# 128-row logit passes, side-by-side compressed blocks and forget gates beside the values in a two-layer hybrid trunk

## The chip, the cores and the metric

The kernel runs on one core of a Trainium2 chip. The metric is device time in microseconds of one execution; the median of three runs of the kernel before is 1275.02 us (1274.71 to 1275.39). Engines are named as in the profile: PE is TensorE's matmul, PEld its load of the stationary operand, DVE is VectorE, ACT ScalarE, POOL GpSimd and SP SyncE, which issues the transfers.

## The reference

A trunk of two layers over 512 positions of width 1024, float32 throughout.

```python
def reference(x, ...):
    h = x
    for layer in range(2):
        hn = rmsnorm(h, mix_norm[layer])
        if layer == 0: h = h + moba_nsa_mixer(hn, ...)
        else:          h = h + fox_mixer(hn, ...)
        h = h + sqrelu_mlp(rmsnorm(h, mlp_norm[layer]), mlp_w1[layer], mlp_w2[layer])
    return rmsnorm(h, final_norm)
```

Layer 0 projects the input once and splits the columns. Eight MoBA heads (width 64) attend causally to blocks of 256 keys, which at 512 positions is causal attention to all keys of the chosen blocks. Eight NSA heads in two key groups have three branches each, weighted by sigmoid gates: compressed keys (31 blocks of 32 positions, stride 16, each pressed through a small MLP `silu(blocks @ w1) @ w2` with hidden width 256), selected blocks and a sliding window. A relative-position bias is added to all these logits. Layer 1 has sixteen forgetting heads: `q k / 8 + cum[q] - cum[k]`, where `cum` is the running sum of `log_sigmoid(h @ w_f + b)` over positions, one column of `w_f` per head. Each mixer ends in an output projection, and an MLP of width 4096 with squared ReLU follows each.

## The kernel before, in words

**Numbers.** Every float32 matrix is split into a rounded part and a rest (`hi` and `lo`, type fp32r), and a product is three matmuls, hi x hi, lo x hi and hi x lo (`mm3`, L129 to L131). `split` (L91 on DVE or POOL, L88 on ACT) makes the two parts of a weight piece of at most 1024 columns per partition; the strings `MIX0_LOW` and `FOX_LOW` say, piece by piece, whether DVE (D) or POOL (P) computes the rest.

**Attention.** For each head, `softmax` (L261) makes the logits of four 128-query rows of 128, 256, 384 and 512 keys. In mixer 0 a row takes two passes over PE: q is stacked as hi in one half of the partitions and lo in the other (`QS`), k as hi in both halves (`KS`), so that one 128-row matmul gives hi x hi + lo x hi. The second pass, hi x lo, uses 64 rows: the hi half of `QS` and the matching half of `KL`, the rest of k. For NSA both halves of `KL` are filled already (`stack_k`, then a DVE subtraction and a POOL rounding), for MoBA one `KL` tile holds the two heads of a pair, one in each half. Then DVE adds the bias and takes the minimum (L265), ACT exponentiates (L266), DVE inverts the sum (L267), POOL normalizes (L268), PE transposes in pieces of 128 (L283), ACT and DVE split the result into `PTh` and `PTl` (L285, L286), and PE multiplies by the values (L295, L296). Probability tiles `P` come from a pool of three, transposed ones from pools of two, PSUM tiles `s`, `pt`, `o`, `acc` from two banks each.

**The compressed branch.** `compress_blocks` builds, for k and for v, the 31 blocks of both groups as 16 chunks of 62 columns, with a rounded tile `rh` and a rest `rl`. `compress_hidden` multiplies each chunk (a stationary tile of 128 columns, of which 62 count) by the weights of 256 columns in three passes. `compress_act` applies SiLU to the 62 x 256 result and transposes it; `compress_out` makes compressed keys `kcc` and values `vcs`, the values repeated in four strips of 32 partitions, one for each head of the group. `cmp_probs` computes the compressed softmax of four heads at once in a tile `cb` of its own. In `nsa_pair` each head multiplies its strip of 32 partitions by `vcs` (L510, L511, 32-row matmuls at a tile position).

**The forget gates.** `forget` in layer 1 loads the 16 gate columns (L951), pads them with zeros to 128 per chunk, splits them (L954, L955) and projects them like the queries, 24 matmuls of 512 columns with `fzh` and `fzl`. It then adds the bias, takes the logarithm and the running sum, and writes rows to memory (`fox_rows`) that the heads' `Q2` and `K2` tiles (68 rows) read. `values(0)`, which stands just before it in `FOX_ORDER`, projects the first 256 value columns for four position tiles.

**Order.** `MIX0_CMP`, `MIX0_ORDER` and `FOX_ORDER` give the order in which the parts are written. A scheduler of the framework then places the instructions on each engine by data, free buffers and priority; attention heads have a high one, so that projections and output projections fill in between. Each engine works its queue in that order.

Of the kernel before, what the change touches and what calls it, by code (L numbers as in the profile page):

```python
# [33 lines left out]
FOX_LOW = "DDPDDDPPPDPDPDDDDPPDPDDDPDPDPDPDD"  # L34
# [11 lines left out]
class Trunk:  # L46
# [278 lines left out]
    def band_setup(self, pool):  # L325

        nc, I = self.nc, self.I
        rb = self.sm.tile([32, 16], F32, tag="rb", name="rb")
        nc.sync.dma_start(rb, I["rel_bias"])
        tb = self.sm.tile([33, 16], F32, tag="tb", name="tb")  # L330
# [42 lines left out]

    def flat(self, v):
        return v.rearrange("p a b -> p (a b)")

    def mixer0(self):
# [5 lines left out]
        with ExitStack() as cx:  # L383
# [5 lines left out]
            self.pL = pool("l0L", 5)  # L389
# [49 lines left out]
            vcs = [a1.tile([P, 2, HD], FR, tag=f"vc{g}", name=f"vc{g}") for g in range(2)]  # L439
            nk = {}  # L440
            with tc.tile_pool(name="cmp", bufs=1) as cp:
# [17 lines left out]
                def nsa_k():  # L459
# [6 lines left out]
                    for g, r in enumerate((lo, hi)):  # L466
                        o_ = hi if g == 0 else lo
                        for bi in range(2):
                            ks = self.stack_k(pss[bi], r)
                            kl = self.pL.tile([P, S], FR, tag="KL", name=self.nm("KL"))  # L470
                            self.sub(kl[r], pss[bi][r], ks[r])
                            self.round(kl[o_], kl[r].bitcast(F32))
                            nk[bi, g] = (ks, kl)

                for s in MIX0_CMP.split():
# [9 lines left out]
                    else:  # L485
# [4 lines left out]
                        if part == 1:  # L490
                            hid[c] = self.compress_act(hid[c], cp)
                self.compress_out((hid[0], hid[1]), cp, kcc, vcs)
            vcf = [self.flat(v) for v in vcs]
# [6 lines left out]
            def nsa_pair(g, i, qs, ptc):  # L500
                o = o2.tile([P, S], F32, tag="o", name=self.nm("o"))
                for jj, r in enumerate((lo, hi)):
                    j = 2 * i + jj
                    head = 4 * g + j
                    with self.prio():
                        b = self.band(8 + head)
                        po = self.psum("o")
                        rr = slice(32 * j, 32 * j + 32)
                        tp = (32 * j, 0)
                        nc.tensor.matmul(po, vcf[g][rr], ptc[0][rr], start=True, stop=False, tile_position=tp)  # L510
                        nc.tensor.matmul(po, vcf[g][rr], ptc[1][rr], start=False, stop=False, tile_position=tp)  # L511
# [8 lines left out]
            def moba_qk(i):  # L520
# [8 lines left out]
                with self.tc.high_priority(offset=0):  # L529
                    ks = [self.stack_k(psk, r) for r in (lo, hi)]  # L530
                    kl = self.pL.tile([P, S], FR, tag="KL", name=self.nm("KL"))
# [4 lines left out]
            def moba_pair(i, qs, ks, kl):  # L536
# [45 lines left out]
    def compress_blocks(self, rg, c, cp):  # L582
# [12 lines left out]
        rh = self.pPT.tile([P, PTW], FR, tag="PTh", name=self.nm("rh"))  # L595
# [481 lines left out]
```

## Time and profile before

| | |
|---|---|
| median of three runs | 1275.02 us |
| the profiled execution | 1274.85 us, its span 1273.1 us |
| granted TensorE clock, mean | 0.997 |
| mixer 0 | 0 to about 332 us of the span |
| first MLP | to about 674 us |
| forgetting layer | to about 920 us |
| second MLP and final norm | to the end |
| busy in the span | PE 1244.3, DVE 957.4, ACT 656.5, POOL 457.9 us |

The profile is of one execution. A row of the timeline gives the start in us from the span's beginning, the duration, the engine, the line, the operation, the written tile <- the read tiles, and for PE the rows * columns of the stationary tile and the moving operand's shape; in brackets stands the idle time before it and what ended it. Matmuls overlap, so their durations add up to more than the time that passes: what one costs is read from the next one's start. A row of the windows gives the stretch, its length, then for each engine the busy time and number of instructions, the granted clock, and the transfers' share and rate. A row of waits names who waited for whom, the total in us, how often, and the longest.

### The profile page before, as it was taken

The page shows a single profiled execution, that of the slowest core. Times are in us where ns is not written, and L with a number is a line of the kernel's source. Part 1 is how long each engine was busy: PE and PEld are TensorE (multiplying, and loading weights), DVE is VectorE, ACT ScalarE, POOL GpSimd, SP SyncE. Part 2 cuts the span into 40 slices and gives each one's busy share as a digit, 9 for nine tenths or more (in the row PEclk, how much of TensorE's full clock was granted, in tenths as well). Part 3 has the DMA queues.
Part 4 walks back from the last instruction along what each step waited for, and adds up shares of the span by engine and source line. Part 5 has one row for each costly group of instructions (what it writes and reads, how often), then busy time and mean ns, then how long its engine had stood idle before and what let it go on. Part 6 is the DMA issues. An engine that isn't in the chain of part 4 may idle for free.

```text
span 1273.1 us, 17191 instructions
## 1 busy us (share of the span) xinstructions
PE 1244.3 (98%) x6254; PEld 1033.7 (81%) x6254; DVE 957.4 (75%) x1626; ACT 656.5 (52%) x1168; POOL 457.9 (36%) x462
## 2 busy tenths in 40 slices
PE   6999999999999999999999999999999999999996
PEld 6787877677888888888888889898798888888885
DVE  6766567767887889888877576647897888889885
ACT  5435565666465544554524676545455445444543
POOL 1534535443253332333201554525326233332313
PEclk9999999999999999999999999999999999999999
DMA  9762132122243332343205212222344324332301
GB/s 264 248 201 70 50 103 72 51 61 90 72 128 115 100 113 87 98 118 113 68 3 136 75 52 68 70 83 67 116 119 130 100 83 133 99 96 88 99 1 66
DMA packets 142048, 124.30 MB, mean 98 GB/s; under 512 B 6363, under 2 KB 116987, under 8 KB 141964
## 3 DMA queue, kind: packets, MB, share of 16 engines
q1 hardware_dynamic: 141964, 123.21, 32.8%
q8 instruction: 49, 0.80, 0.3%
q14 instruction: 35, 0.29, 0.1%
HBM read 120.79 MB, written 7.64 MB: 101 GB/s over the span
## 4 chain that ended last, share of the span: by engine, by line
PE 95%; DVE 3%; ACT 1%; DMA 0%; issue 0%; SPq 0%; DVEq 0%; ACTq 0%
PE acc L129 18%; PE acc L131 18%; PE acc L130 18%; PE s L856 12%; PE o L856 6%; PE s L261 6%; PE pt L283 4%; PE pt L856 3%; PE o L295 2%; PE o L296 2%; PE pt L232 1%; DVE whl L91 1%; PE s L131 1%; PE s L129 1%; PE s L130 1%; PE o L130 1%
## 5 line engine op out<-in xcount | busy, mean ns | idle before, releaser
L131 PE MATMUL acc<-xhi,whl 128*128 128x512 f32 (+1 forms) x784 | 301.0, 384 | 0.0
L130 PE MATMUL acc<-xlo,whl 128*128 128x512 f32 (+1 forms) x784 | 300.2, 383 | 0.0
L129 PE MATMUL acc<-xhi,whl 128*128 128x512 f32 (+1 forms) x784 | 299.9, 383 | 0.0
L91 DVE TENSOR_TENSOR whl<-raw,whl 128x1024 fp32r<-128x1024 f32 (+1 forms) x112 | 156.7, 1402 | 77.1 <-ACT whl L88 72.7
L759 POOL TENSOR_TENSOR r<-r,yrow 128x512 f32<-128x512 f32 x64 | 93.9, 1467 | 321.5 <-ACT r L758 319.1
L129 PEld LDWEIGHTS acc<-xhi,whl 128*128 128x128 f32 x784 | 147.4, 188 | 28.8 <-issue 1.3
L131 PEld LDWEIGHTS acc<-xhi,whl 128*128 128x128 f32 x784 | 147.5, 188 | 28.3 <-issue 0.5
L130 PEld LDWEIGHTS acc<-xlo,whl 128*128 128x128 f32 x784 | 147.6, 188 | 28.0 <-issue 0.7
L856 PE MATMUL s<-whl,sp 128*128 128x512 f32 x672 | 168.0, 390 | 0.0
L88 ACT ACTIVATE whl<-raw 128x1024 fp32r<-128x1024 f32 (+1 forms) x143 | 149.3, 1048 | 31.4 <-PE acc L131 11.8
L856 PEld LDWEIGHTS s<-whl,sp 128*128 128x128 f32 x672 | 126.2, 188 | 26.3
L811 DVE TENSOR_TENSOR whl<-w,whl 128x1024 fp32r<-128x1024 f32 x98 | 136.0, 1400 | 8.5 <-ACT whl L810 8.4
L810 ACT ACTIVATE whl<-w 128x1024 fp32r<-128x1024 f32 x98 | 102.4, 1059 | 72.6 <-PE s L856 42.3
L266 ACT ACTIVATE P<-P,sst 128x128 f32<-128x128 f32 (+3 forms) x160 | 88.9, 557 | 49.0 <-DVE sst L265 48.5
L758 ACT ACTIVATE r<-acc 128x512 f32<-128x512 f32 x62 | 37.1, 598 | 120.9 <-PE acc L131 120.9
L816 DVE TENSOR_TENSOR w<-w,w 128x1024 f32<-128x1024 f32 x56 | 91.2, 1629 | 9.0 <-DMA w<-in_mlp_w 8.1
L91 POOL TENSOR_TENSOR whl<-raw,whl 128x1024 fp32r<-128x1024 f32 (+2 forms) x31 | 75.1, 2425 | 62.8 <-ACT whl L88 51.2
L285 ACT ACTIVATE PTh<-pt 128x512 fp32r<-128x512 f32 (+1 forms) x120 | 61.3, 524 | 60.2 <-PE pt L283 58.9
L286 DVE TENSOR_TENSOR PTl<-pt,PTh 128x512 fp32r<-128x512 f32 (+1 forms) x120 | 70.5, 597 | 25.6 <-ACT PTh L285 24.7
L856 PE MATMUL o<-whl,sp 128*128 128x512 f32 x336 | 88.8, 390 | 0.0
L864 DVE TENSOR_TENSOR x<-s,x 128x512 f32<-128x512 f32 x112 | 75.1, 681 | 3.0 <-PE s L856 3.0
L268 POOL TENSOR_SCALAR P<-P,sst 128x128 f32<-128x128 f32 (+1 forms) x96 | 51.9, 546 | 67.5 <-DVE sst L267 66.1
(226 smaller groups left out, 2417.5 us busy)
## 6 DMA issues: line engine op xcount, KB each, us to landing
raw<-in_mlp_w SPq DMA_DIRECT2D x72, 512.0 KB
w<-in_mlp_w SPq DMA_DIRECT2D x56, 512.0 KB
raw<-in_odd_w_in SPq DMA_DIRECT2D x24, 512.0 KB
raw<-in_even_w_in SPq DMA_DIRECT2D x20, 512.0 KB
band<-bias_dram SPq DMA_DIRECT2D x24, 256.0 KB
bias_dram<-bias_rows SPq DMA_DIRECT2D x16, 320.0 KB
raw<-in_even_w_out SPq DMA_DIRECT2D x8, 512.0 KB
raw<-in_odd_w_out SPq DMA_DIRECT2D x8, 512.0 KB
```

What stands on the lines that cost most here:

```text
L88: i0 = nc.scalar.activation(hl[:, 0, :n], raw[:, :n], AF.Copy)
L91: i1 = eng.tensor_tensor(hl[:, 1, :n], raw[:, :n], hl[:, 0, :n].bitcast(F32), op=ALU.subtract)
L129: mm(ps, ahl[0], bhl[0], start=first, stop=False)
L130: mm(ps, ahl[0], bhl[1], start=False, stop=False)
L131: mm(ps, ahl[1], bhl[0], start=False, stop=last)
L261: nc.tensor.matmul(ps[:, :w], q[:, qi * P:(qi + 1) * P], k[:, :w], start=i == 0, stop=i == len(passes) - 1)
L266: nc.scalar.activation(seg, seg, AF.Exp, bias=mn, scale=-1.0, accum_out=sm)
L759: nc.gpsimd.tensor_tensor(r, r, row, op=ALU.mult)
L810: nc.scalar.activation(t[:, 0], src, AF.Copy)
L811: nc.vector.tensor_tensor(t[:, 1], src, t[:, 0].bitcast(F32), op=ALU.subtract)
L816: nc.vector.tensor_tensor(out, a_, b_, op=op)
L856: mm = lambda l, r, first, last: nc.tensor.matmul(ps, l, r, start=first, stop=last, skip_group_check=True)
```

## The change

Four things change.

1. The second logit pass in mixer 0 uses all 128 rows: `QS` (hi and lo halves) against a `KL` tile that holds the rest of k in both halves, so that lo x lo is added too. A helper `stack_kl` makes such a tile for each head; MoBA pairs have two tiles instead of one, and their pool grows from five to six. To make room, `cb` comes from the pool of probability tiles, and small tiles move to other pools.
2. In the compressed branch the rounded part and the rest of a chunk stand side by side in one stationary tile (62 + 62 columns), so that two passes (weights hi, weights lo) make four products. The two halves of the result are added after the transposition, in `compress_act`, and SiLU follows there.
3. The compressed values are laid out per head as 128 rows, zero outside the head's strip, so that the 32-row matmuls become 128-row ones without a tile position.
4. The forget gates' 16 columns are loaded with the first 256 value columns (three weight pieces instead of two) and projected with them, 272 columns; the 16 gate columns are copied to `zt` and transposed (L966) for the rest of `forget`.

```diff
-FOX_LOW = "DDPDDDPPPDPDPDDDDPPDPDDDPDPDPDPDD"
+FOX_LOW = "DDDPDDDPPPDPDPDDDDPPDPDDDPDPDPDPDD"
...
+    def stack_kl(self, ps, r, ks):
+        o = slice(HD, P) if r.start == 0 else slice(0, HD)
+        kl = self.pL.tile([P, S], FR, tag="KL", name=self.nm("KL"))
+        self.sub(kl[r], ps[r], ks[r])
+        self.round(kl[o], kl[r].bitcast(F32))
+        return kl
...
-            self.pL = pool("l0L", 5)
+            self.pL = pool("l0L", 6)
...
-                        rr = slice(32 * j, 32 * j + 32)
-                        tp = (32 * j, 0)
-                        nc.tensor.matmul(po, vcf[g][rr], ptc[0][rr], start=True, stop=False, tile_position=tp)
-                        nc.tensor.matmul(po, vcf[g][rr], ptc[1][rr], start=False, stop=False, tile_position=tp)
+                        nc.tensor.matmul(po, vcf[g][j], ptc[0], start=True, stop=False)
+                        nc.tensor.matmul(po, vcf[g][j], ptc[1], start=False, stop=False)
...
-                            p = self.softmax([(qs[j], ks), (qs[j][r], kl[r])], b, gates[:, :, 3 * head + 1 + bi])
+                            p = self.softmax([(qs[j], ks), (qs[j], kl)], b, gates[:, :, 3 * head + 1 + bi])
...
-                    kl = self.pL.tile([P, S], FR, tag="KL", name=self.nm("KL"))
-                    for r, k in zip((lo, hi), ks):
-                        self.sub(kl[r], psk[r], k[r])
-                return qs, ks, kl
+                    kls = [self.stack_kl(psk, r, k) for r, k in zip((lo, hi), ks)]
+                return qs, ks, kls
...
-                        p = self.softmax([(qs[j], ks[j]), (qs[j][r], kl[r])], b, None)
+                        p = self.softmax([(qs[j], ks[j]), (qs[j], kls[j])], b, None)
...
-        self.round(rh[:, :W + 66], rf[:, :W + 66])
-        nc.vector.tensor_tensor(rl[:, :W + 66], rf[:, :W + 66], rh[:, :W + 66].bitcast(F32), op=ALU.subtract)
-        return rh, rl
+        for hh, t in enumerate(rhl):
+            nc.gpsimd.memset(t[:, V:V + 4].bitcast(F32), 0.0)
+            tv = t[:, :V].rearrange("p (c h n) -> p c h n", c=8, h=2)
+            src = rf[:, hh * V // 2:(hh + 1) * V // 2].rearrange("p (c n) -> p c n", c=8)
+            self.round(tv[:, :, 0], src)
+            nc.vector.tensor_tensor(tv[:, :, 1], src, tv[:, :, 0].bitcast(F32), op=ALU.subtract)
+        return rhl
...
-            self.mm3(ps[:, :256], (rh[:, a], rl[:, a]), wc[k], cc == 0, cc == 15)
+            a = blocks[part][:, k * 124:k * 124 + P]
+            mm(ps[:, :256], a, wc[k][0], start=cc == 0, stop=False)
+            mm(ps[:, :256], a, wc[k][1], start=False, stop=cc == 15)
...
+        sg = cp.tile([124, 256], F32, tag="sg", name=self.nm("sg"))
+        nc.scalar.activation(sg, ps[:124, :256], AF.Copy)
...
+        nc.scalar.activation(z, pv[:, :, 62:124], AF.Copy)
+        nc.vector.tensor_tensor(z, pv[:, :, :62], z, op=ALU.add)
+        nc.scalar.activation(e, z, AF.Exp, scale=-1.0)
...
+            nc.gpsimd.memset(vcs[g].bitcast(F32), 0.0)
+            for j in range(4):
+                r = slice(32 * j, 32 * j + 32)
+                nc.scalar.activation(vcs[g][r, j, 0], pvv[r, :HD], AF.Copy)
+                self.sub(vcs[g][r, j, 1], pvv[r, :HD], vcs[g][r, j, 0])
...
-        cb = b1.tile([P, 4, 4, 32], F32, tag="cb", name=self.nm("cb"))
+        cb = self.pP.tile([P, PTW], F32, tag="P", name=self.nm("cb"))[:, :S].rearrange("p (q h n) -> p q h n", q=4, h=4)
...
-            wv = self.cols(w, [(2048, 2304)])
+            wv = self.cols(w, [(2048, 2304), (3072, 3088)])
...
-                    self.proj_n(ps, wc, 256, x, t)
+                    self.proj_n(ps, wc, 272 if c == 0 else 256, x, t)
+                    if c == 0:
+                        nc.vector.tensor_copy(zt[:, t], ps[:, 256:272])
...
-                nc.vector.tensor_tensor(fl, fr, fh.bitcast(F32), op=ALU.subtract)
-                psz = self.psum("acc")
-                for k in range(KD):
-                    self.mm3(psz, (fh[:, k], fl[:, k]), (x[0][:, k], x[1][:, k]), k == 0, k == KD - 1)
+                psz = self.psum("pt")
+                for t in range(NT):
+                    nc.tensor.transpose(psz[:16, t * P:(t + 1) * P], zt[:, t], self.ident)
```

The change moves few instructions. On PE the order of the attention heads stays the same but for one place, the MoBA heads at the time of the second compressed softmax. These are PE's rows there before, from a head's first product with the values (`vm`) on; `s` are logits, `acc` a projection:

```order
L296 MATMUL o_1968<-PTl_1948,vm_249 128x512
L131 MATMUL acc_2249<-xhi_122,whl_2246 128x512
L129 MATMUL acc_2249<-xhi_122,whl_2246 128x512
L130 MATMUL acc_2249<-xlo_123,whl_2246 128x512
L261 MATMUL s_2117<-KS_1651,QS_1615 128x128
L261 MATMUL s_2117<-KL_1657,QS_1615 128x128
L261 MATMUL s_2124<-KS_1651,QS_1615 128x256
L261 MATMUL s_2124<-KL_1657,QS_1615 128x256
```

And now the rows that stand between the last of the 18 projection matmuls that follow the same product and the head's first logits:

```order
L130 MATMUL acc_2288<-xlo_123,whl_2285 128x512
L295 MATMUL o_1971<-PTh_1950,vm_250 128x384
L131 MATMUL acc_2288<-xhi_122,whl_2285 128x512
L129 MATMUL acc_2288<-xhi_122,whl_2285 128x512
L283 MATMUL pt_2016<-ident,P_1984 128x128 x4
L296 MATMUL o_1971<-PTl_1951,vm_250 128x384
L283 MATMUL pt_2023<-ident,P_1984 128x128 x4
L295 MATMUL o_1971<-PTh_1950,vm_252 128x128
L296 MATMUL o_1971<-PTl_1951,vm_252 128x128
L295 MATMUL o_1971<-PTh_1950,vm_251 128x256
L296 MATMUL o_1971<-PTl_1951,vm_251 128x256
L261 MATMUL s_2120<-KS_1651,QS_1615 128x128
```

The head's logits (`QS_1615`) stood three projection matmuls behind that product and now stand behind 20 of them and the rest of the previous head.

At the forgetting layer's start DVE has these rows before, between the last two additions of the MLP (L898) and the third normalized tile:

```order
L955 TENSOR_TENSOR fzl<-fzr,fzh 128x1024
L898 TENSOR_TENSOR x_120<-o_6060,x_120 128x512
L171 SCALAR_TENSOR_TENSOR nrm_6164<-nrm_6164 128x1
L91 TENSOR_TENSOR whl_6100<-raw_6095,whl_6100 128x1024
L237 TENSOR_TENSOR xlo_6106<-pt_6121,xhi_6105 128x4x128
L237 TENSOR_TENSOR xlo_6106<-pt_6128,xhi_6105 128x4x128
L204 SCALAR_TENSOR_TENSOR xn_6163<-x_118,nrm_6164,g_6103 128x512 x2
```

And now, from the last addition (L909) on:

```order
L909 TENSOR_TENSOR x_120<-o_6069,x_120 128x512
L91 TENSOR_TENSOR whl_6114<-raw_6105,whl_6114 128x816
L91 TENSOR_TENSOR whl_6117<-raw_6108,whl_6117 128x544
L237 TENSOR_TENSOR xlo_6123<-pt_6138,xhi_6122 128x4x128
L237 TENSOR_TENSOR xlo_6123<-pt_6145,xhi_6122 128x4x128
```

The split of the gate weights (`fzl`) is gone, and two of the three smaller value pieces stand ahead of the normalized input's rest (`xlo`) in place of one.

More of the change, by code (lines that the diff above doesn't have):

```diff
@@ L327, in band_setup @@
         nc, I = self.nc, self.I
[L328 removed]
+        rb = pool.tile([32, 16], F32, tag="rb", name="rb")
         nc.sync.dma_start(rb, I["rel_bias"])
[L330 removed]
+        tb = pool.tile([33, 16], F32, tag="tb", name="tb")
         nc.vector.memset(tb, -NEG)
@@ L438, in mixer0 @@
             kcc = a1.tile([P, 2, 2, 2, 32], FR, name="kcc")
-            vcs = [a1.tile([P, 2, HD], FR, tag=f"vc{g}", name=f"vc{g}") for g in range(2)]
+            vcs = [a1.tile([P, 4, 2, HD], FR, tag=f"vc{g}", name=f"vc{g}") for g in range(2)]
             nk = {}
@@ L490, in mixer0 @@
                         if part == 1:
-                            hid[c] = self.compress_act(hid[c], cp)
+                            hid[c] = self.compress_act(hid[c], c, cp)
                 self.compress_out((hid[0], hid[1]), cp, kcc, vcs)
-            vcf = [self.flat(v) for v in vcs]
+            vcf = [[self.flat(v[:, j]) for j in range(4)] for v in vcs]
             self.pB = pool("l0B", 2)
@@ L594, in compress_blocks @@
         rf = self.pP.tile([P, PTW], F32, tag="P", name=self.nm("rf"))
-        rh = self.pPT.tile([P, PTW], FR, tag="PTh", name=self.nm("rh"))
-        rl = self.pPT.tile([P, PTW], FR, tag="PTl", name=self.nm("rl"))
-        nc.gpsimd.memset(rf[:, W:W + 66], 0.0)
+        rhl = [self.pPT.tile([P, PTW], FR, tag=tg, name=self.nm("rhl")) for tg in ("PTh", "PTl")]
+        V = 8 * 4 * NB
         rv = rf[:, :W].rearrange("p (c g n) -> p c g n", c=16, g=2)
@@ L640, in compress_out @@
             w2.append(t)
-        hkt = cp.tile([P, 2, 62], F32, name="hkt")
-        for f in range(2):
-            nc.vector.tensor_copy(hkt[:, f], hk[:, f * P:f * P + 62])
         pk = self.psum("o")
         for f in range(2):
-            nc.tensor.matmul(pk[:, :62], w2[0][:, f], hkt[:, f], start=f == 0, stop=f == 1)
+            nc.tensor.matmul(pk[:, :62], w2[0][:, f], hk[:, f], start=f == 0, stop=f == 1)
         nc.vector.memset(kcc.bitcast(F32), 0.0)
@@ L689, in cmp_probs @@
                 nc.vector.tensor_tensor(cbh, src, cbh, op=ALU.add)
-        st = self.sm.tile([P, 2, 16], F32, tag="cst", name=self.nm("cst"))
+        st = b1.tile([P, 2, 16], F32, tag="cst", name=self.nm("cst"))
         cv = cb.rearrange("p q h n -> p (q h) n")
@@ L946, in forget @@
                 ft = lambda pool_, tag, name, dt: pool_.tile([P, PTW], dt, tag=tag, name=name)
-                kv = lambda t_: t_[:, :KD * P].rearrange("p (k c) -> p k c", k=KD)
-                fr, fh, fl = (kv(ft(p_, t_, n_, d_)) for p_, t_, n_, d_ in (
-                    (self.pP, "P", "fzr", F32), (self.pPT, "PTh", "fzh", FR), (self.pPT, "PTl", "fzl", FR)))
-                nc.gpsimd.memset(fr, 0.0)
-                nc.sync.dma_start(fr[:, :, :16], w.rearrange("(k p) c -> p k c", p=P)[:, :, 3072:3088])
                 bf = a1.tile([16, 1], F32, name="bforget")
                 nc.sync.dma_start(bf, I["odd_b_forget"][0].rearrange("(h o) -> h o", o=1))
-                nc.scalar.activation(fh, fr, AF.Copy)
-                nc.vector.tensor_tensor(fl, fr, fh.bitcast(F32), op=ALU.subtract)
-                psz = self.psum("acc")
-                for k in range(KD):
-                    self.mm3(psz, (fh[:, k], fl[:, k]), (x[0][:, k], x[1][:, k]), k == 0, k == KD - 1)
+                psz = self.psum("pt")
+                for t in range(NT):
+                    nc.tensor.transpose(psz[:16, t * P:(t + 1) * P], zt[:, t], self.ident)
                 ze = ft(self.pP, "P", "ze", F32)
```

33 lines of the change are left out of this document (14 added, 19 removed).

## The prediction

> **What bounds the kernel now.** First the page: busy time and the chain of waits.
>
> ```profile
> span 1273.1 us, 17191 instructions
> PE 1244.3 (98%) x6254; PEld 1033.7 (81%) x6254; DVE 957.4 (75%) x1626; ACT 656.5 (52%) x1168; POOL 457.9 (36%) x462
> PE 95%; DVE 3%; ACT 1%; DMA 0%; issue 0%; SPq 0%; DVEq 0%; ACTq 0%
> ```
>
> TensorE ends nearly every wait. Busy PE is not yet useful PE, though, because a matmul's row includes its pipeline's tail. So next comes the timeline, where what counts is the distance from one start to the next. Here is a stretch of mixer 0 that contains logit rows (KS,QS is the first pass, KL,QS the second, 64 rows), and then one of the forgetting layer.
>
> ```profile
> 201.79 0.36 PE L296 MATMUL o<-PTl,vm 128*128 128x256 f32 x1
> 202.08 0.44 PE L261 MATMUL s<-KL,QS 64*128 64x384 f32 x1
> 202.46 0.50 PE L261 MATMUL s<-KS,QS 128*128 128x512 f32 x1
> 202.89 0.50 PE L261 MATMUL s<-KL,QS 64*128 64x512 f32 x1
> 203.32 0.50 PE L130 MATMUL acc<-xlo,whl 128*128 128x512 f32 x1
> 203.65 0.40 PE L131 MATMUL acc<-xhi,whl 128*128 128x512 f32 x1
> ...
> 720.95 0.97 PE L261 MATMUL s<-K,Q 128*128 128x384 f32 x4
> 721.76 0.40 PE L131 MATMUL acc<-xhi,whl 128*128 128x512 f32 x1
> 721.99 0.39 PE L129 MATMUL acc<-xhi,whl 128*128 128x512 f32 x1
> ```
>
> A 512-column matmul between others of 128 rows takes 0.23 us (721.76 to 721.99). The four logit matmuls of the forgetting layer (two of 384 columns, two of 512) take 0.81 us, so 384 columns take (0.81 - 0.46)/2 = 0.175 us. In mixer 0 the matmuls that start at 202.08 should then end at 202.08 + 0.175 + 3 x 0.23 = 202.95; the next one starts at 203.65. So 0.70 us are lost around two 64-row passes: 0.35 us each, half of it before the next 128-row pass, half before the 64-row pass. Third, the chain of waits of the two attention stretches (95 to 330, then 690 to 920), the windows, and who waits in mixer 0.
>
> ```profile
> by line: PE s L261 21.7%; PE acc L129 15.8%; PE acc L130 15.2%; PE acc L131 15.1%; PE pt L283 12.7%; PE o L295 7.6%; PE o L296 7.3%; PE o L510 1.3%; DVE x L322 0.9%; PE o L511 0.8%; PE s L674 0.7%; PE pt L705 0.4%; DVE o L302 0.3%; ACT o L3
> by line: PE acc L129 24.4%; PE acc L131 24.2%; PE acc L130 24.2%; PE s L261 8.7%; PE pt L283 7.7%; PE o L296 4.4%; PE o L295 4.3%; DVE whl L91 1.2%; issue 0.6%; DVE x L322 0.3%; PE pt L232 0.1%; DVEq L91 0.0%; DVEq L223 0.0%
> 95.00:320.00 225.00, 225.00 (x1168) 172.12 (x1167) 150.96 (x449) 134.49 (x327) 99.66 (x145) 1.00 0.24 71
> DVE P L265 <- PE s L261: 32.7, 36, 4.3
> ACT PTh L285 <- PE pt L283: 38.9, 31, 4.0
> PEld s L261 <- issue: 15.5, 67, 0.4
> ```
>
> L261 is 21.7% of 235 us, 51.0 us for 96 pairs of passes, against 8.7% of 230 us, 20.0 us for 64 pairs: 0.53 us a pair against 0.31. From 95 to 320 PE never stops, and VectorE (150.96) and ScalarE (134.49 of 225) wait for it. That stretch is bound by PE, and part of its PE time is the passage between tile heights.
>
> **The 128-row logit passes.** 96 64-row matmuls become 96 of the same width with 128 rows. The forgetting layer's passes have 128 and 68 rows by turns and pay only for columns, so the added rows cost nothing and the gain is the lost time. From the chain it is 0.22 us a pair, 21.0 us; from starts 0.35, 33.6 us; with the wait ahead of the first of them (201.79 to 202.08 is 0.29 where 256 columns should take 0.12, rows below) it is 0.70 + 0.17 for two passes, 0.44, or 42 us. I take 33.6, because starts are measured and the chain's ends are modelled, and because neighbouring pairs share a passage. The whole will not come out: where softmaxes stand without projections between them, the vector engines come next.
>
> ```profile
> 230.00:240.00 10.00, 10.00 (x43) 6.08 (x42) 7.71 (x29) 6.84 (x20) 7.22 (x8) 1.00 0.43 134
> 280.00:300.00 20.00, 20.00 (x101) 13.80 (x101) 14.88 (x62) 15.83 (x46) 8.83 (x16) 1.00 0.24 64
> ...
> 230.00:240.00 10.00, 4.99 (x14) 2.66 (x14) 1.00 0.43 134
> 280.00:300.00 20.00, 10.63 (x33) 6.15 (x33) 1.00 0.24 64
> ...
> 674.00:690.00 16.00, 12.85 (x95) 12.21 (x93) 14.19 (x26) 7.48 (x13) 4.60 (x4) 0.89 0.56 149
> ```
>
> The second pair of rows counts L261 alone: 33 passes in 280 to 300, so 16.5 x 0.35 = 5.8 us to be had, leaving 14.2 us of PE against 15.83 of ScalarE. How full can an engine get? From 674 to 690, where VectorE holds up PE, it was busy for 14.19 of 16 us, 89%. By that, 280 to 300 shrinks to 15.83/0.89 = 17.8, 3.6 us less than hoped; 230 to 240 shrinks to 7.71/0.89 = 8.7 instead of 7.55, 1.1 us less. Over the whole stretch VectorE's 151 would be 79% of 225 - 34 us, below that. Another 2.3 us I take off as an estimate (half of 18 x 0.23 = 4.1 us) for the softmax that the order moves behind 18 projection matmuls: it comes out later, where there is less cover. What is left: 33.6 - 7.0 = **26.6 us**.
>
> This part adds eight rounds of KL on POOL and a KL tile per head. The nearest row:
>
> ```profile
> L250 POOL TENSOR_SCALAR KL<-KL 64x512 fp32r<-64x512 f32 x4 | 5.1, 1272 | 0.6 <-DVE KL L244 0.3
> ```
>
> 8 x 1.27 = 10 us on an engine with 99.66 of 225 busy; the first logits of a MoBA head wait for it, with the projections as cover. Without that cover it would be 1.3 us a head. I price it at nothing, up to 10. The smaller tiles that change pools (bias table, statistics) are written once and cost nothing.
>
> **32-row passes.** 16 matmuls against the compressed values take 1.3% + 0.8% of 235 = 4.9 us, 0.31 each; 16 x 0.23 = 3.7. Gain **1.2 us**. Against this stands the pair that the next rows show.
>
> ```profile
> 111.23 0.50 PE L510 MATMUL o<-ptch,vc 32*128 32x512 f32 x2
> 111.66 0.33 PE L283 MATMUL pt<-ident,P 128*128 128x128 f32 x1
> ```
>
> Two matmuls of different 32-row strips finished in 0.43 us, as long as two of 128 rows one after the other (0.46). The Trainium skill ("TensorE: Matmul & The Clock Gate", Part 3) has matmuls in distinct row strips run concurrently, four of 32 rows 3.07 times as fast; that speaks against giving the strips up. By that page the two pairs that stand side by side would save 0.23 us each and the change would give back some 0.5 us. By the rows here they save 0.03: the passage in and out eats the overlap. The added part (ScalarE and VectorE write the values in eight 32-row pieces each, two zero fills on POOL) is 12 more instructions of about 0.22 us in the shadow of the query projections.
>
> **Compressed blocks.** 48 matmuls of 256 columns for k and for v become 32.
>
> ```profile
> 53.53 0.28 PE L130 MATMUL o<-whl,rh 128*128 128x256 f32 x1
> 53.65 0.28 PE L131 MATMUL o<-whl,rl 128*128 128x256 f32 x1
> 57.42 0.39 PE L130 MATMUL o<-whl,rh 128*128 128x256 f32 x1 [0.90 <-DVE whl L91]
> 61.91 0.39 PE L130 MATMUL o<-whl,rh 128*128 128x256 f32 x1 [1.38 <-POOL whl L91]
> 65.92 0.33 PE L627 MATMUL pt<-ident,sg 62*128 62x62 f32 x2 [0.90 <-DVE sg L624]
> ```
>
> 32 x 0.12 = 3.8 us less PE. But PE waits here for split weights, so most of this only lengthens those waits; the weight tiles come free a little sooner. The wait for the activation (0.90) goes, because the transposes now come before the sigmoid, after one copy. Between 0 and 3.8 + 0.9, nearer the waits: **2.0 us**.
>
> **Forget gates.** The separate projection goes, 24 matmuls of 512 columns; 16 columns are added to 96 matmuls of the first value projection, and four transposes.
>
> ```profile
> 694.10 0.40 PE L129 MATMUL acc<-xhi,fzh 128*128 128x512 f32 x1
> 694.34 0.40 PE L130 MATMUL acc<-xlo,fzh 128*128 128x512 f32 x1
> ...
> 673.74 1.23 DVE L955 TENSOR_TENSOR fzl<-fzr,fzh 128x1024 fp32r<-128x1024 f32 x1 [0.42 <-ACT fzh L954]
> 677.42 1.12 PE L232 MATMUL pt<-ident,xn 128*128 128x128 f32 x4 [1.73 <-DVE xlo L237]
> 678.55 0.41 PE L129 MATMUL acc<-whl,xhi 128*128 128x256 f32 x1
> 678.76 0.41 PE L130 MATMUL acc<-whl,xhi 128*128 128x256 f32 x1
> ```
>
> 24 x 0.23 = 5.5 us go. A column costs (0.23 - 0.12)/256 = 0.43 ns, so 96 x 16 of them cost 0.66, and four transposes (0.11 each, an estimate from the 256-column step) 0.44: 4.4 us. At the layer's start VectorE holds up PE, and the forget weights' split of 1.23 us sits in its queue ahead of the work that PE waits for at 677.42; it goes, while the first value weights come in three pieces instead of two with 6% more columns, and four small copies are added, together some 0.8 us (estimate: 0.06 x 2.5, one start, 4 x 0.1). I count **4.8 us** in all. The small loads of 16 columns now stand ahead of the norm row on SP's queue, issued early enough behind the last MLP weights; if not, up to 1 us comes back. The clock too: PE at 678.55 took 0.21 us a matmul, not 0.12 (granted clock 0.89); that spell of ten matmuls, 0.9 us, may vanish or move. So 3.0 to 6.5.
>
> **Sum.** 26.6 + 1.2 + 2.0 + 4.8 = 34.6 us, from the profiled execution's 1274.85 (span 1273.1 and 1.75 around it, 0.17 under the median): 1240.3, and with the 0.17, 1240.4; I say **1241**.
>
> **Rivals.** (1) All of it comes out, since softmaxes still overlap and ScalarE's queue fills to the brim: 36 + 1.2 + 3.5 + 5.5 = 46, 1229. For it: VectorE and ScalarE wait for PE for 32.7 and 38.9 us; against: the 280 to 300 window. (2) The vector engines' latency takes over wherever softmaxes are dense, and the chain's 21.0 is the true price, less 7: 14 + 1.2 + 1 + 4.5 = 21, 1254. For it: ScalarE at 79% there; against: the starts. (3) The loss belongs to the operands KS and QS, not to the 64 rows, and stays: 1.2 + 2 + 4.8, 1267. Against it: the row after a 64-row pass loses too, though it reads neither. (4) Slower: the compressed softmax now takes one of the three probability tiles.
>
> ```profile
> L682 POOL COPY cb<-band x32: 191/210/233, 86.8 to 189.3; 128x7 f32<-128x7 f32 x8, 128x15 f32<-128x15 f32 x8, 128x23 f32<-128x23 f32 x8, 128x31 f32<-128x31 f32 x8
> L705 PE MATMUL pt<-ident,cb x8: 272/272/330, 105.7 to 210.3; 128*128 128x128 f32 x8
> ```
>
> Group 0 would hold it from 86.8 to 106, 19 us, and group 1 as long. If PE stood still throughout with nothing to put in, 38 us would go: 1274.85 - 34.6 + 38 = 1278. It decides from 35 us of such waits on; 18 projection matmuls stand in the first of these gaps, so it is unlikely.
>
> **Numbers.** Forecast 0.62, (1) 0.14, (2) 0.16, (3) 0.04, (4) 0.04. The range 1229 to 1256 holds the forecast, the near side of (1) and (2). 0.2% (2.5 us) is about what can be told from no change: faster 0.95, within 0.02, slower 0.03, the rest of (4) being a partial stall.
>
> **What would show it.** In the changed profile L261 should fall to about 9% to 14% of the chain from 95 to 290, with starts 0.23 us apart after a 512-column KL pass; L619 and L620 count 64; no fzh matmuls; VectorE near 80% from 95 to 285. New PE waits for DVE or ACT inside mixer 0 of more than 10 us would make it (2); POOL naming KL or cb ahead of PE would be (4). A start 0.43 us after a 128-row KL pass would make the main term wrong.

## The result, and the profile after

The changed kernel takes 1241.27 us, the median of four runs (1240.76 to 1242.59), against 1275.05 us before (1274.71 to 1275.39): a ratio of 0.9737, with an interval of 0.972 to 0.9754, or 33.8 us less. The forecast was 1241, with a range of 1229 to 1256. The profiled execution is the slowest of the four, 1242.59 us. Its page (span, busy time, the chain of waits by engine):

```profile
span 1240.9 us, 17121 instructions
PE 1206.7 (97%) x6202; PEld 1023.9 (83%) x6202; DVE 955.6 (77%) x1638; ACT 655.0 (53%) x1178; POOL 465.1 (37%) x475
PE 88%; DVE 5%; ACT 2%; issue 2%; DMA 1%; POOL 1%; SPq 0%; POOLq 0%; DVEq 0%; ACTq 0%
```

PE's busy time fell by 37.6 us, that of the other engines stayed within 8 us of what it was. PE still ends most waits, but 88% and no longer 95%: the vector engines now come up in the chain.

**Where the time went, by stage.** A stage is cut at the first PE transpose of a layer's normalized input (L232). From the timelines of before and after:

```profile
332.66 1.04 PE L232 MATMUL pt<-ident,xn 128*128 128x128 f32 x8
921.53 0.27 PE L232 MATMUL pt<-ident,xn 128*128 128x128 f32 x1
```

```profile
303.48 1.04 PE L232 MATMUL pt<-ident,xn 128*128 128x128 f32 x8
644.61 1.03 PE L232 MATMUL pt<-ident,xn 128*128 128x128 f32 x8
889.37 0.38 PE L232 MATMUL pt<-ident,xn 128*128 128x128 f32 x2
```

Before, the forgetting layer's own row stood at 673.79. So mixer 0 took 332.66 us and takes 303.48 (29.2 less), the first MLP 341.13 in both, the forgetting layer 247.74 and now 244.76 (3.0 less), and the rest is the same to 0.1 us. By the prediction's terms mixer 0 should give 26.6 + 1.2 + 2.0 = 29.8 and the forgetting layer 4.8.

**The logit passes.** A timeline of mixer 0 after, then from 95 to 290 the chain of waits by line, and the windows of 95 to 285:

```profile
203.59 0.40 PE L261 MATMUL s<-KS,QS 128*128 128x512 f32 x1
203.82 0.39 PE L261 MATMUL s<-KL,QS 128*128 128x512 f32 x1
204.06 0.40 PE L129 MATMUL acc<-whl,O 128*128 128x512 f32 x1
204.29 0.40 PE L130 MATMUL acc<-whl,O 128*128 128x512 f32 x1
```

```profile
by line: PE acc L129 12.2%; PE acc L130 11.7%; PE acc L131 11.7%; PE s L261 11.6%; PE pt L283 11.1%; PE o L296 6.1%; PE o L295 5.4%; issue 4.0%; DVE P L265 3.6%; DMA band<-bias_dram 3.4%; DVE KL L244 2.1%; DVE PTl L286 2.0%; POOL whl L91 1.
95.00:285.00 190.00, 187.08 (x1139) 163.74 (x1137) 147.82 (x450) 128.32 (x321) 104.38 (x154) 1.00 0.29 86
```

All starts are 0.23 us apart, also around the KL pass (203.82, 204.06): the passage between tile heights is gone. L261 fell from 21.7% of the chain to 11.6%, VectorE's share of the stretch rose to 147.82/190 = 78%. Who waits, from 95 to 300:

```profile
POOL P L268 <- DVE sst L267: 59.4, 51, 4.0
ACT PTh L285 <- PE pt L283: 20.4, 16, 3.6
DVE P L265 <- PE s L261: 15.0, 17, 2.9
PE s L261 <- DVE sst L265: 1.0, 3, 0.7
```

The vector engines still wait for PE, about half as long as before (32.7 and 38.9 us then, over a longer stretch). PE itself, for which the profile of before shows no wait from 95 to 304, now waits 3.4 us there in all, 1.0 of them at the logits. That is far from the 10 us that rival 2 would need, and no row names POOL's `KL` or `cb` ahead of PE.

**The compressed blocks**, 50 to 75 us, PE's waits after, and the windows of 53.4 to 70 before and after (16.6 us each):

```profile
PE o L620 <- POOL whl L91: 2.6, 2, 1.7
PE o L620 <- DVE whl L91: 1.5, 2, 1.0
PE o L619 <- ACT whl L88: 0.6, 1, 0.6
PE pt L629 <- ACT sg L626: 0.5, 1, 0.5
```

```profile
53.40:70.00 16.60, 13.42 (x106) 12.63 (x105) 14.23 (x14) 10.75 (x14) 11.11 (x8) 1.00 0.71 202
```

```profile
53.40:70.00 16.60, 11.44 (x74) 9.36 (x73) 13.89 (x12) 10.65 (x14) 11.07 (x8) 1.00 0.63 175
```

PE is busy for 2 us less of the same 16.6, and waits for 5.2 us, 4.7 of them for split weights; before, the three waits shown made 3.2, 2.3 of them for split weights. VectorE's busy time is nearly the same, and from 55.3 on it hardly pauses (after; before it was busy for 14.67 of the same 16.2):

```profile
55.30:71.50 16.20, 11.04 (x72) 8.97 (x71) 15.35 (x13) 11.33 (x16) 11.07 (x8) 1.00 0.67 179
```

Part of this busy time goes with what POOL does: in the changed kernel's profile VectorE's split of 1024 columns (L91) takes 1.22 us in the median where POOL does not subtract at the time, and up to 3.24 us beside a subtraction on POOL. **The forgetting layer's start**, PE's waits from 643 to 685 after:

```profile
PE pt L232 <- DVE xlo L237: 1.7, 2, 1.5
PE acc L131 <- POOL whl L91: 0.8, 1, 0.8
PE acc L129 <- ACT xhi L236: 0.7, 2, 0.4
PE acc L129 <- DVE Q L246: 0.5, 1, 0.5
```

The waits for `xlo` are shorter (1.73 and 1.05 us before). The others are new or longer: for the first query weight's split on POOL, for `xhi` (0.4 before) and for `Q`. Before, the separate gate projection stood there on PE.

**The program's start** was not touched, and still it differs. PE's timelines before and after, the first value projection of 280 columns:

```profile
14.87 0.42 PE L129 MATMUL acc<-whl,xhi 128*128 128x280 f32 x1
15.10 0.33 PE L130 MATMUL acc<-whl,xhi 128*128 128x280 f32 x1
15.27 0.29 PE L131 MATMUL acc<-whl,xlo 128*128 128x280 f32 x1
15.40 0.29 PE L129 MATMUL acc<-whl,xhi 128*128 128x280 f32 x1
```

```profile
16.96 0.43 PE L129 MATMUL acc<-whl,xhi 128*128 128x280 f32 x1
17.19 0.42 PE L130 MATMUL acc<-whl,xhi 128*128 128x280 f32 x1
17.43 0.32 PE L131 MATMUL acc<-whl,xlo 128*128 128x280 f32 x1
```

The same instructions start 0.23 us apart until 15.1 in one execution and until 17.4 in the other, and 0.125 apart from then on: 10 slow matmuls against 20, 1.05 us. More on this at the end; it has to be taken out before stages are compared.

### The profile page after: what moved, and what is told of

The parts are those of the page before. It is cut to its first block, busy times and chain, and to the rows that moved or that the text cites. A ratio compares the mean times of both kernels' runs of the same rounds, so it can differ in the third digit from the quotient of the medians.

```text
span 1240.9 us, 17121 instructions
## 1 busy us (share of the span) xinstructions
PE 1206.7 (97%) x6202; PEld 1023.9 (83%) x6202; DVE 955.6 (77%) x1638; ACT 655.0 (53%) x1178; POOL 465.1 (37%) x475
## 4 chain that ended last, share of the span: by engine, by line
PE 88%; DVE 5%; ACT 2%; issue 2%; DMA 1%; POOL 1%; SPq 0%; POOLq 0%; DVEq 0%; ACTq 0%
PE acc L129 17%; PE acc L131 17%; PE acc L130 17%; PE s L867 12%; PE o L867 6%; PE s L261 3%; PE pt L283 3%; PE pt L867 3%; PE o L296 2%; PE o L295 2%; DVE whl L91 1%; PE pt L232 1%; DMA band<-bias_dram 1%; PE s L131 1%; PE s L129 1%
## 5 line engine op out<-in xcount | busy, mean ns | idle before, releaser
L91 DVE TENSOR_TENSOR whl<-raw,whl 128x1024 fp32r<-128x1024 f32 (+2 forms) x113 | 158.7, 1409 | 74.3 <-ACT whl L88 61.9
L131 PEld LDWEIGHTS acc<-xhi,whl 128*128 128x128 f32 x784 | 147.6, 188 | 29.2 <-POOL whl L91 1.2
L821 ACT ACTIVATE whl<-w 128x1024 fp32r<-128x1024 f32 x98 | 102.4, 1059 | 69.9 <-PE s L867 42.8
L91 POOL TENSOR_TENSOR whl<-raw,whl 128x1024 fp32r<-128x1024 f32 (+2 forms) x31 | 74.5, 2404 | 83.2 <-ACT whl L88 60.9
```

Source lines behind the costliest of these rows:

```text
L91: i1 = eng.tensor_tensor(hl[:, 1, :n], raw[:, :n], hl[:, 0, :n].bitcast(F32), op=ALU.subtract)
L131: mm(ps, ahl[1], bhl[0], start=False, stop=last)
L821: nc.scalar.activation(t[:, 0], src, AF.Copy)
```

## Experiments

All times are medians; a kernel's ratio is to the kernel before on the same chip, with its interval. The runs used several chips, on which the kernel before had medians from 1275.05 to 1277.64 us, so that whole times of two runs compare to a microsecond or two. What a part is worth was then read by stages, as above, since the whole time also carries what the scheduler and the clock do elsewhere.

### Undoing one part at a time

**The logit passes.** Only the second pass goes back to 64 rows; not one PE instruction changes its place.

```diff
-p = self.softmax([(qs[j], ks), (qs[j], kl)], b, ...)
+p = self.softmax([(qs[j], ks), (qs[j][r], kl[r])], b, ...)
```

> The changed kernel with only the second logit pass of mixer 0 back at 64 rows (the matching halves of QS and KL); the order of all instructions stays the same. Changed kernel: 1241.3 us. Theory (each 64-row pass costs 0.35 us in passages, part of it hidden by vector engines that are behind): 26.6 us come back by the prediction, 29 by the comparison of the two traces, so 1268 to 1271. Rival 2 (the chain's price, less 7): 14 us, 1255. Rival 3 (the loss belongs to the operands, not to the height): 1241.

Measured: 1268.01 us, ratio 0.9944 (0.9932 to 0.9957). Mixer 0 takes 330.36 us against 303.48, so 26.9 us come back, 27.2 with the start evened out (17 slow matmuls against 20). That is the prediction's 26.6. Rivals 2 and 3 are out.

Because the order is the same, the start of the same PE instruction can be compared in both runs, and the loss read piece by piece. The last columns are the same comparison between the runs *m7* and *m5* below, in which VectorE has less to do (the 64-row run cut at the same times to 0.3 us).

| stretch with 64 rows, us | same stretch with 128 rows | passes | longer by, us | a pass | *VectorE relieved:* passes | a pass |
|---|---|---|---|---|---|---|
| 90 to 110 | 90.3 to 108.9 | 5 | 1.46 | 0.29 | 5 | 0.32 |
| 110 to 131 | 108.9 to 126.8 | 12 | 3.13 | 0.26 | 13 | 0.32 |
| 131 to 201 | 126.8 to 188.2 | 24 | 8.63 | 0.36 | 24 | 0.35 |
| 201 to 222 | 188.2 to 207.0 | 8 | 2.10 | 0.26 | 8 | 0.29 |
| 222 to 242 | 207.0 to 224.1 | 14 | 3.16 | 0.23 | 12 | 0.31 |
| 242 to 272 | 224.1 to 250.1 | 11 | 3.87 | 0.35 | 12 | 0.35 |
| 272 to 303 | 250.1 to 276.1 | 22 | 4.78 | 0.22 | 22 | 0.28 |
| sum | | 96 | 27.1 | 0.28 | 96 | 0.32 |

Where projections stand between the softmaxes a pass costs 0.35 us; where softmaxes are dense (222 to 242, 272 to 303) it costs 0.22. The windows of such a piece, first with 64 rows, then the same work after:

```profile
282.30:302.70 20.40, 20.40 (x106) 14.48 (x106) 16.73 (x64) 17.32 (x50) 10.04 (x18) 1.00 0.18 46
```

```profile
258.70:275.80 17.10, 16.49 (x108) 13.98 (x107) 16.17 (x66) 16.43 (x49) 9.65 (x17) 1.00 0.24 64
```

ScalarE is busy for 16.43 of 17.1 us, 96%, VectorE for 95%, and PE no longer fills the stretch: here the vector engines are the likely bound. They get fuller than the 89% of the prediction.

**The compressed blocks.** Three passes for each chunk, and the old activation, as in the diff of the change read backwards.

> The changed kernel with only the compressed blocks back at three passes per chunk and the old activation. By the prediction 2.0 us come back (1243.3), by full PE time and the activation's wait 4.7 (1246.0). By the traces the stretch only waits longer for its split weights, so nothing comes back: 1241, give or take 1.

Measured: 1242.23 us, ratio 0.9739 (0.9725 to 0.9752). Mixer 0 takes 302.46 us, with 12 slow matmuls at the start; with 20 it would be 303.3, against 303.48. This part is worth nothing.

**The 32-row matmuls.** `vcs` again holds the values in four strips of 32 partitions, and `nsa_pair` multiplies one of them.

```diff
-nc.tensor.matmul(po, vcf[g][j], ptc[0], start=True, stop=False)
+nc.tensor.matmul(po, vcf[g][rr], ptc[0][rr], start=True, stop=False, tile_position=(32 * j, 0))
```

> The changed kernel with only the matmuls against the compressed values back at 32 rows and a tile position. By the prediction 1.2 us come back: 1242.5. If the strips that stand side by side run at the same time, the 32-row form is 0.5 us better: 1240.8. If each passage from and to a 32-row strip costs as much as one to 64 rows (16 x 0.35), up to 5.6 us come back: 1247.

Measured: 1242.65 us, ratio 0.9743 (0.9729 to 0.9756). Mixer 0 takes 305.14 us with the same 20 slow matmuls at the start: 1.7 us more than with 128 rows. In the profiled execution the forgetting layer was 1.5 us shorter than in that of the changed kernel, for a reason that has nothing to do with the strips (see the clock, at the end). The forecast was 1.2. PE's instructions and their order are the same in both kernels but for the 16 matmuls themselves. Twelve of the 16 come as hi and lo of one strip, alone among 128-row work:

```profile
135.13 0.49 PE L515 MATMUL o<-ptch,vc 32*128 32x512 f32 x1
135.47 0.39 PE L516 MATMUL o<-ptcl,vc 32*128 32x512 f32 x1
135.79 0.39 PE L130 MATMUL acc<-whl,xhi 128*128 128x256 f32 x1
```

At these six places the run falls behind the changed kernel by 1.9 us in all, about 0.3 each. The Trainium skill ("TensorE: Matmul & The Clock Gate", Part 3) would have strips side by side run at the same time, which spoke for keeping them. The other four matmuls, two strips at a time, do start together (both at 109.65 us, the next matmul 0.42 us later, the same again at 110.33), and the run gains 0.3 us there. But the changed kernel waits for its data at that place (0.30 and 0.24 us), so a gain from the overlap is not shown.

**The forget gates.** `forget` loads, splits and projects its own weights again.

> The changed kernel with only the separate projection of the forget gates back. By the prediction 4.8 us come back: 1246.1. By the traces 3.0, since a new wait for a split weight (0.83 us on POOL) stands where the projection was: 1244.3.

Measured: 1243.2 us, ratio 0.9744 (0.9731 to 0.9758). The forgetting layer takes 245.94 us. That profile has no spell of slow matmuls at the layer's start; profiles of the changed layer without one have 243.2 us (the run before this one and four below), with one 244.7. So this part is worth 2.7 us, not 4.8. PE's waits from 644 to 685 with the projection in place:

```profile
PE pt L232 <- DVE xlo L237: 1.7, 1, 1.7
PE acc L129 <- ACT xhi L236: 0.4, 1, 0.4
PE acc L131 <- DVE xlo L237: 0.2, 1, 0.2
```

2.3 us in all, against 3.7 us in the four rows shown of after.

### Part 1 alone

> The kernel before (1275.4 us) with part 1 alone: the 128-row logit passes, the KL tile and POOL rounding per head, and the pools that make room for them; the compressed blocks, the 32-row matmuls and the forget gates stay as before. By the prediction 26.6 us faster: 1248.8. If, as undoing the parts one by one suggests (27 for part 1, 2.7 for the gates, 1.7 for the 32-row matmuls, 0 for the blocks), parts add up, 27 to 28.5 us: 1247 to 1248.5. If the POOL rounds or the lent probability tile cost something that undoing hid, less: 1250 or more.

Measured: 1246.25 us, ratio 0.9762 (0.9748 to 0.9777). Mixer 0 takes 304.89 us against 332.66 before, with nearly the same start (12 and 10 slow matmuls): 28.0 us. Here the order of the instructions changes too, the moved MoBA head and the lent probability tile included, and no loss by them shows in the sum. The parts do not quite add up: 304.89 to 303.48, with the starts evened out, leaves 2.3 us in mixer 0 for parts 2 and 3, where undoing them one by one gave 1.7 and nothing.

### Is it the height of the tile?

The forgetting layer's second pass has 68 rows. Cut to 64, it should lose what mixer 0 gained, though its operands and its order have nothing of mixer 0.

```diff
-p = self.softmax([(q1, k1), (q2, k2)], band, None)
+p = self.softmax([(q1, k1), (q2[lo], k2[lo])], band, None)
```

> The changed kernel (1241.3 us) with the second logit pass of the forgetting layer cut from 68 to 64 rows, so that the four rows with the gates' running sums are left out of the product; the order of all instructions stays the same. Theory (a pass of 64 rows among 128-row work costs 0.35 us of passage, whatever its operands): 64 x 0.35 = 22.4 us slower, 1264. If the loss belongs to mixer 0's operands or order: 1241, since a pass is paid by columns.

Measured: 1262.62 us, ratio 0.9899 (0.9885 to 0.9913), 21.4 us more than the changed kernel, for 64 passes with four rows fewer. The layer's logits, after and in this run (count, then shortest, median and longest in ns, first and last start):

```profile
L261 PE MATMUL s<-K,Q x128: 219/335/476, 683.7 to 865.6; 128*128 128x128 f32 x16, 128*128 128x256 f32 x16, 68*128 68x128 f32 x16, 68*128 68x256 f32 x16
```

```profile
L261 PE MATMUL s<-K,Q x128: 219/380/507, 681.9 to 885.7; 128*128 128x128 f32 x16, 128*128 128x256 f32 x16, 64*128 64x128 f32 x16, 64*128 64x256 f32 x16
```

From first to last it takes 203.8 us instead of 181.9, 21.9 us for 64 passes, and to the layer's end 22.2: 0.35 us each, the prediction's price to the second figure. A matmul of 68 rows costs what one of 128 costs, and one of 64 rows among them costs 0.35 us more.

### What holds back the rest

33.3 us (96 x 0.347) could come out in mixer 0, 27.2 do. The next run (*m5*) takes VectorE's low part of the probabilities out of mixer 0 and multiplies the high part twice (`transpose_p`, for mixer 0 alone).

```diff
-nc.vector.tensor_tensor(lo[...], pt[...], hi[...].bitcast(F32), op=ALU.subtract)
-return hi, lo
+return hi, hi
```

> The changed kernel (1241.3 us) without VectorE's computation of the low part of the transposed probabilities in mixer 0: the high part is multiplied twice, so that TensorE has the same work, VectorE loses three instructions a head. Theory (some 7 us of the 33.6 are held back by the vector engines where softmaxes stand close): up to 7 us faster, 1234 to 1238. If TensorE alone bounds mixer 0 now (rival 1's reason): no change, 1241.

Measured: 1238.18 us, ratio 0.9707 (0.9694 to 0.972), 3.1 us less than the changed kernel. PE has the same matmuls, but not quite in the same order: about one in nine stands elsewhere. Its windows from 95 to 285 (after: VectorE 147.82, ScalarE 128.32):

```profile
95.00:285.00 190.00, 189.03 (x1161) 166.41 (x1160) 117.12 (x382) 129.99 (x325) 102.48 (x150) 1.00 0.28 85
```

31 us less on VectorE give 2.7 us from the first logits to the end of mixer 0. To see whether these belong to the hidden passages, the same kernel with 64-row passes, in the same order (*m7*):

> The kernel of the run without VectorE's low part of the probabilities in mixer 0 (high part multiplied twice; 1238.2 us, 3.1 under the changed kernel), and with the second logit pass of mixer 0 back at 64 rows; the order of its instructions is the same as in that run. Theory (in the changed kernel the vector engines hold back some 6 of 33 us of passages, VectorE about 3 of them): with VectorE relieved the 64-row form costs 30 us instead of 27, so 1268, as much as with VectorE unrelieved, because with 64 rows TensorE bounds either way. Rival (the relief is worth 3 us whatever bounds, by order or latency at the edges): 27 us, 1265.

Measured: 1270.37 us, ratio 0.9959 (0.9945 to 0.9972). In the profiles mixer 0 takes 330.95 us against 300.52 in *m5*, with equal starts (10 and 11 slow matmuls): 30.4 us, 0.32 a pass (last column of the table). With 64 rows the relief of VectorE changes nothing (from the first logits to the end of mixer 0 232.4 us, 231.9 unrelieved), with 128 rows it gives 2.7. So VectorE holds back about 3 of the 6 us, unless a part of these 3 belongs to the order, which differs between this pair of runs and the pair without relief. The other 3 stay where softmaxes are densest (0.28 a pass from 272 to 303); ScalarE's 96% there makes it the likely holder, but no run relieved ScalarE.

### POOL's roundings of KL

```diff
 self.round(kl[o], kl[r].bitcast(F32))
+self.round(kl[o], kl[r].bitcast(F32))
```

> The changed kernel (1241.3 us) with each POOL rounding of KL done twice in place (12 more of 1.3 to 1.7 us). By the prediction's price of nothing for these rounds: 1241 to 1242. If the logits of a head wait for POOL: up to 12 x 1.3 = 16 us slower, and POOL named ahead of PE's logits.

Measured: 1242.88 us, ratio 0.9738 (0.9722 to 0.9755). Mixer 0 takes 303.09 us with 15 slow matmuls at the start, 303.6 evened out, against 303.48. Two views of it, the roundings and PE's waits from 95 to 305:

```profile
L250 POOL TENSOR_SCALAR KL<-KL x24: 612/614/1699, 50.4 to 256.4; 64x512 fp32r<-64x512 f32 x24
PE o L296 <- DVE PTl L286: 0.8, 1, 0.8
PE acc L129 <- DVE x L322: 0.7, 2, 0.5
```

Twelve more roundings (0.61 us in the median, up to 1.7; the prediction had 1.27) cost nothing that can be measured, and no wait of PE names them.

### Attempts to get more

**The query weight's split on VectorE.** One letter of `FOX_LOW`, the fourth, from P to D.

> The changed kernel (1241.3 us) with the low part of the forgetting layer's first query weights computed by VectorE instead of POOL (one letter of FOX_LOW). Theory (the separate gate projection was the cover of that split, and its wait of 0.83 us is new): 0.8 us less from the layer's start to its first logits (39.1 to 38.3); whole time 1240.5. If VectorE's own queue takes its place: no change.

Measured: 1242.34 us, ratio 0.9736 (0.9722 to 0.9749): no change. POOL's wait is gone, and the layer's first logits start 35.8 us after the layer's start instead of 37.6 in the profiles without a spell there (39.1 in the changed kernel's, with one). That is 1.8 us earlier, and fits the theory that the gate projection had covered this split. But the layer takes 245.54 us, and the windows tell why (the granted clock is the third figure from the end of a row):

```profile
679.59:690.00 10.41, 9.46 (x43) 6.92 (x41) 5.29 (x19) 6.83 (x13) 6.82 (x7) 1.00 0.47 120
690.00:694.00 4.00, 4.00 (x11) 3.14 (x12) 2.27 (x11) 2.97 (x11) 3.82 (x8) 0.57 0.48 135
```

The softmaxes came early, PE filled 679.6 to 690 less well, and from 690.5 to 693.5 its 512-column matmuls start 0.43 us apart instead of 0.23, which with the edges costs 1.6 us. From its first logits on the layer takes 4.1 us more than in the profiles without a spell: 1.6 by the clock, the rest with the new order of its instructions. What the wait had given is lost again, and 2.3 us more.

**Another piece on VectorE in the compressed blocks.** Letters 12 to 15 of `MIX0_LOW` from PDPD to DPDP.

> The changed kernel (1241.3 us) with two pairs of weight pieces of the compressed blocks changing engines: the first piece of each pair is split by VectorE, the second by POOL (in the changed kernel the other way round; the order of the other instructions stays nearly the same). Theory: TensorE waits 0.9 and 1.7 us there for POOL's first pieces, which take 2.4 us against 1.2; with the second piece on POOL the split runs while TensorE works on the first, so 1 to 2 us faster: 1239.5 to 1240.5. If the vector engines' total in that stretch bounds it: no change.

Measured: 1241.9 us, ratio 0.973 (0.9716 to 0.9745). PE's waits there are now

```profile
PE o L620 <- POOL whl L91: 2.8, 1, 2.8
PE o L620 <- DVE whl L91: 1.0, 1, 1.0
```

with the two small ones as before: 4.9 us instead of 5.2, and the last of these matmuls starts 1.7 us later. The waits move, their sum stays. In this profile the granted clock is 0.51 from 64.1 to 71.0, where these matmuls start 0.21 us apart instead of 0.12; how much earlier the last one would come without that, the run does not show.

**Work between the compressed branches.** The first query projection is written between them.

```diff
-MIX0_CMP = "c1 c0 b k h00 h01 h10 h11 q"
+MIX0_CMP = "c1 c0 b k h00 h01 q h10 h11"
```

> The changed kernel (1241.3 us) with the first NSA query projection written between the two compressed branches instead of behind them. Theory (the compressed blocks save 3.4 us of TensorE work and wait 3.4 us more for split weights, and other TensorE work put there covers the waits): 2 to 4 us faster, 1237 to 1239. If the vector engines' total of splitting bounds the whole stretch to the first logits: no change, 1241.

Measured: 1247.21 us, ratio 0.9777 (0.9764 to 0.979), 5.9 us slower than the changed kernel. PE's waits from 60 to 110:

```profile
PE s L261 <- DVE cb L700: 4.0, 1, 4.0
PE acc L131 <- DVE whl L91: 3.2, 2, 1.9
PE o L620 <- DVE whl L91: 0.7, 1, 0.7
```

The projection waits for its own split weights instead, and the compressed values are finished so late (the last compressed matmul at 80.5 instead of 69.9) that PE then stands still for the first compressed softmax. The chain runs over the bias: SP issues the bands (`band`, L355) only when the compressed values' last matmul (L669, 89.2 us) is done, POOL waits for them before it fills `cb` (9.8 us in all), VectorE adds the compressed logits to it (L700), and PE waits for the PSUM tile in which these logits stand. Behind that wait the clock drops (SP's wait, then a window):

```profile
SPq L355 <- PE o L669: 4.3, 1, 4.3
98.00:105.20 7.20, 4.51 (x12) 3.61 (x13) 6.62 (x16) 3.30 (x8) 6.00 (x6) 0.53 0.69 201
```

From the start of the first to that of the last of eight 512-column matmuls it takes 3.1 us there instead of 1.6, so about 1.5 of the 5.9 us are the clock's. VectorE is busy for 20.1 of 30 us from 60 to 90 and is not what bounds this order. None of the three attempts beats the changed kernel.

## Why the prediction was right, step by step

**The bound and the price of a passage: right.** The loss belongs to 64-row tiles among 128-row ones, 0.35 us a pass. The same price came out of the forgetting layer, where nothing hides it. The signs that were named came too: L261 at 11.6% of the chain, starts 0.23 us apart, 64 matmuls on L619 and L620, VectorE at 78%, and 3.4 us of new waits of PE, not 10.

**128-row logit passes, 26.6 us: right in size (27.2 undone, 28.0 alone), partly wrong in its deduction.** 7.0 us were taken off; 6.1 are held back. But of the three pieces the one for the moved softmax (2.3 us; half of its 4.1 is 2.1, so the pieces make 6.8) finds no support: with that move included, part 1 alone gives no less than without it. Instead the two dense stretches are spread wider than the two windows showed: 222 to 242 and 272 to 303 hold back 4.5 us, the stretches from 110 to 131 and 201 to 222 another 1.7. The bound of 89% for a full engine was too low for ScalarE (96%), which made the piece of 3.6 us too large for its stretch (2.9).

**32-row passes, 1.2 us: right, 1.7 measured.** The whole of it comes from the twelve matmuls that stand alone with their strip.

**Compressed blocks, 2.0 us: wrong, nothing.** The working said that PE waits for split weights and that most of the saving would lengthen those waits; the step that failed is the "weight tiles come free a little sooner" and the wait for the activation, 2 us between them. VectorE and POOL have as much to do there as before, and VectorE is busy for 15.35 of 16.2 us, so that tiles that come free sooner bring nothing; and new waits (0.5 and 0.6 us for ScalarE) took the place of the 0.90. That VectorE is the bound there is read from its busy time, and no run relieved it. The lower end of the range was the truth.

**Forget gates, 4.8 us: too large, 2.7.** It lies below its own range (3.0 to 6.5). The work on PE was right: from the layer's start to its first logits the matmuls, counted at 0.23 us for 512 columns, make 35.0 us with the projection and 30.4 without, 4.6 less where 4.4 stood. What failed is the other side of the step: VectorE was to give 0.4 more, and instead what PE takes beyond that rate grew from 5.4 to 7.2 us (in the two profiles of undone parts without a spell), 1.4 of it in the rows shown. The new wait for the first query weight comes because the removed projection had been the work behind which it was split: with that split on VectorE the first logits start 1.8 us earlier. The prediction asked what the removed split on VectorE would free, not what the removed matmuls had covered.

**POOL's roundings, nothing: right**, with half the duration that was priced.

**The sum.** 27.2 + 1.7 + 0 + 2.7 = 31.6 by parts undone. The profiled executions differ by 32.3, or 33.3 with their starts evened out, the medians by 33.8. The 2 us between belong to no single part: the orders that the scheduler makes of each version differ, and undoing a part does not bring back the order of before. 1.3 us of them lie in mixer 0 (30.2 with the starts evened out, 28.9 by parts), and which pieces these are, no run settles. In the forgetting layer one piece can be found: with part 1 alone, which leaves that layer's code as it was, it takes 246.52 us against 247.74 before, since VectorE's rows differ there in the place of one instruction and the second wait for `xlo` (1.05 us) is gone. That the forecast came so close was luck in part: errors of -0.6, -0.5, +2.0 and +2.1 us met these 2 us.

**The rivals.** (1) All comes out: 33.3 us of the main term do not, so no. (2) The chain's 21.0, less 7: no; L261's share of the chain undercounts what starts show. (3) Operands: refuted twice, by undoing the height alone and by the forgetting layer. (4) The lent tile: no wait of PE names `cb` in the changed kernel. The 4.0 us in the run with the queries between are a wait for the PSUM tile of the compressed logits, not for the lent one.

## What to carry to other kernels

Read a matmul's price from the distance between starts: a tile of 64 rows among full ones costs the passage in and out, here more than a whole 512-column matmul, and rows filled with a harmless product are cheaper than rows left out. Before work is removed from the engine that bounds a stretch, ask what is prepared behind it; where that preparation is the real bound, the saved time turns into waits. And compare versions by stages with the clock's spells taken out, since a scheduler's order and the clock move other stages by as much as a small edit.

## What was not expected of the hardware

**The half clock, and its luck.** At the program's start between 10 and 20 of the same 280-column matmuls ran at half speed in the runs above (up to 1.05 us), and at the forgetting layer's start between 0 and 12 (1.5 us: 244.7 us for the changed layer in four profiles with such a spell, 243.2 in five without, *m5* and *m7* among them). In the first 20 us the rows' granted clock stays at 1.00 through it, so that there only the starts show it. The Trainium skill ("TensorE: Matmul & The Clock Gate", Part 1) has the gate decide in windows of about 3.4 us that run freely, so that the number of slow matmuls changes from run to run; these counts agree, and the spells that the granted clock shows inside the kernels last 3.4 or 6.8 us. Eight profiles (*m5* and *m7* among them) have another such spell between 58 and 71 us, where PE waits for split weights; in the run with 32-row matmuls it leaves no delay, and its instructions at 116 us start no later than the changed kernel's. A better-fed layer start can lose its gain to a spell a little later, as the query weight's run did at 690 us.

**68 rows are as good as 128.** The forgetting layer's 68-row passes run among 128-row ones with no loss; at 64 rows the loss is there at once. The Trainium skill ("TensorEngine Tiling (Array Packing)", Key Properties) says that changing the tiling mode drains the engine; it gives no price, and these runs give 0.35 us for the way in and out together.
